# A two-layer block and a second block on one core: gated outputs copied out of PSUM early, decays spread among key projections, sums of squares moved to VectorE, one more value piece ahead of the first transposes

## The chip, the core and the metric

The kernel runs on one core of a Trainium2 chip. Its engines are TensorE (PE in the profile, with its weight loads as PEld), VectorE (DVE), ScalarE (ACT), GpSimd (POOL) and SyncE (SP), which issues most DMAs. Each engine takes its own instructions strictly in order and waits for others by semaphores. The metric is device time in microseconds (us), as a median of several runs.

## The reference

x (512 tokens, 1024 features) goes through two layers of a first block, and then through a second block (windowed attention with a spatial gate, attention over a memory of 256 tokens, a feed-forward part). The change lies in the two layers. Cut to what matters, one layer computes:

```
h = rmsnorm(x);  z = h @ w_in                       # g_q g_k g_v g_lr g_gate  c_q c_kv k_pe  m_gate
log_a = log_sigmoid(g_lr @ w_gate_up + b) / 16      # decays of the gated linear attention (gla)
b = cumsum(log_a) in chunks;  q_dec = q*exp(b);  k_inv = k*exp(-b)
o = causal(q_dec k_inv^T) v + q_dec state           # 4 heads of 64 x 128, state carried from chunk to chunk
o_gla = rmsnorm(o, per head) * silu(g_gate)
q = rmsnorm(c_q) @ w_uq;  k, v = rmsnorm(c_kv) @ w_ukv   # 4 heads, norm per head, rope, causal softmax
o_mla = softmax(q k^T) v * silu(m_gate)
x = x + concat(o_gla, o_mla) @ w_out
```

## The kernel before

Every large product is computed as three fp32r matmuls of a high and a low part (`mm3`, L232 to L234): high by high, low by high, high by low. So every weight is split after its DMA: a ScalarE cast makes the high part (L94, tile whi) and a VectorE subtraction the low part (L95, tile wlo). x is split likewise in `u_chunk` (L360 on ScalarE, L361 on VectorE), which also sums the squares of x over its eight pieces of 128 features: ScalarE squares (L366), and GpSimd adds to `sq` (L367). RMS scales are not applied to x before the product but to its results, so `sq` is only needed when `r_cols` (L378) turns it to one scale per token.

The program is written as one stream, and a scheduler decides from it the order in which each engine's instructions stand, PE's too. What fills PE while a chain of small operations runs elsewhere is handed out by `Fill`: a call runs one piece of a projection (half an output tile, 12 matmuls of 512 columns) and then what is due by `later(d, ...)` after d calls.

Layer 0 begins with `first_proj`: for each of the eight pieces of x, 12 matmuls of 464 columns into four accumulators (three banks of tag s and the one bank of tag o). In the same loop `rope_angles` puts small VectorE operations (L306 to L327) between the pieces. Then `r_cols`, `post_a` (scales and sums of squares of the latents), one value piece, and for each token tile t of 128 tokens `post_b` (the normed latent `cn`, L489 and L491), a value piece and `post_c`, whose transposes (L241) bring the latent of the tile before to feature order. Eight value pieces exist; layer 0 uses five up to here.

Then `queries` for t = 0 to 3 (12 matmuls of 384 columns each; ScalarE's L539 sums squares and frees the bank), with `decays` behind the first (matmul L510, exp L515, log L516, subtraction L518) and value pieces between. Behind the queries of tile t stands `gla_decay(t - 1)`: a matmul with a cumulative mask into the o bank (L613), two exponentials out of it (L615, L616) and a copy (L617). `r_bcast` (L390, copied by L392) spreads the scales. Then `keys` for t = 0 to 3, each two matmul groups into banks of tag s, with pieces of the gla projections between.

`attention` runs the softmax attention (`mla_scores`: matmuls L717 and L720 into two banks of tag s), and inside its fills the gla chunks: `gla_scores`, and one call later `gla_out`, which accumulates into two banks `po` (L666, L672). There are three banks of tag s in all. `po` is squared (L695), reduced (L696), turned to a scale (GpSimd's power, L246), and one call later multiplied out of PSUM (L702); only then are the two banks free.

## Time and profile before

| | |
|---|---|
| median of 3 runs | 1286.16 us (1284.43 to 1286.36) |
| the profiled execution: its time, its span | 1282.27 us, 1280.6 us |
| instructions | 16386 |
| DVE busy | 718.1 us (56%) |
| ACT busy | 519.9 us (41%) |
| POOL busy | 218.6 us (17%) |
| granted TensorE clock, mean | 0.997 |

Shares of busy time are averages over stages with different limits. The chain that ended last lists the lines of `mm3` first, each at 19% of the span. In the view by stretches of 20 us, PE is below 19.99 us busy in the stretches up to 160 us and from 280 to 420 us, at 580, 680, 860 and 880 us, and at the end; these first two ranges are the two layers up to the end of their attention.

### The profile page before, as it was taken

The page shows a single profiled execution, that of the slowest core. Times are in us where ns is not written, and L with a number is a line of the kernel's source. Part 1 is how long each engine was busy: PE and PEld are TensorE (multiplying, and loading weights), DVE is VectorE, ACT ScalarE, POOL GpSimd, SP SyncE. Part 2 cuts the span into 40 slices and gives each one's busy share as a digit, 9 for nine tenths or more (in the row PEclk, how much of TensorE's full clock was granted, in tenths as well). Part 3 has the DMA queues.
Part 4 walks back from the last instruction along what each step waited for, and adds up shares of the span by engine and source line. Part 5 has one row for each costly group of instructions (what it writes and reads, how often), then busy time and mean ns, then how long its engine had stood idle before and what let it go on. Part 6 is the DMA issues. An engine that isn't in the chain of part 4 may idle for free.

```text
span 1280.6 us, 16386 instructions
## 1 busy us (share of the span) xinstructions
PE 1255.0 (98%) x6158; PEld 1020.3 (80%) x6158; DVE 718.1 (56%) x1372; ACT 519.9 (41%) x1174; POOL 218.6 (17%) x247
## 2 busy tenths in 40 slices
PE   8899999999999999999999999999999999999997
PEld 6786678888766888888888888887888888888886
DVE  8666566566656554545376447646655543555532
ACT  6663334456433442215643334445433222333231
POOL 4442001344210141000010002200311100011110
PEclk9999999999999999999999999999999999999999
DMA  6123014513302375221123333323222224332311
GB/s 226 60 100 101 34 33 144 175 46 99 115 1 66 109 229 189 68 98 67 63 78 92 101 95 107 99 99 99 99 86 96 72 90 131 104 97 97 105 48 66
DMA packets 39375, 124.32 MB, mean 97 GB/s; under 512 B 4812, under 2 KB 5862, under 8 KB 39168
## 3 DMA queue, kind: packets, MB, share of 16 engines
q1 hardware_dynamic: 36432, 114.18, 27.4%
q0 software_dynamic: 2576, 8.79, 2.2%
q8 instruction: 48, 0.79, 0.2%
q10 hardware_dynamic: 288, 0.31, 0.1%
q14 instruction: 31, 0.25, 0.1%
HBM read 116.97 MB, written 6.29 MB: 96 GB/s over the span
## 4 chain that ended last, share of the span: by engine, by line
PE 65%; DVE 2%; issue 1%; ACT 1%; POOL 0%; POOLq 0%; ACTq 0%; DVEq 0%
PE psz L232 19%; PE psz L233 19%; PE psz L234 19%; PE pstr L241 1%; PE pss L232 1%; PE pss L234 1%; PE pss L233 1%; PE pss L1142 1%; PE pss L1475 1%; PE pso L755 0%; PE pso L1274 0%; PE pss L717 0%; DVE wlo L95 0%; POOL sm L246 0%; PE pss L1514 0%
## 5 line engine op out<-in xcount | busy, mean ns | idle before, releaser
L94 ACT CAST whi<-wraw 128x512 fp32r<-128x512 f32 (+4 forms) x420 | 226.4, 594 | 311.8 <-PE psz L233 228.0
L95 DVE TENSOR_TENSOR wlo<-wraw,whi 128x512 fp32r<-128x512 f32 (+4 forms) x420 | 298.4, 753 | 70.7 <-ACT whi L94 69.6
L232 PE MATMUL psz<-u,whi 128*128 128x512 f32 x768 | 303.4, 395 | 0.0
L234 PE MATMUL psz<-u,wlo 128*128 128x512 f32 x768 | 299.7, 390 | 0.0
L233 PE MATMUL psz<-u,whi 128*128 128x512 f32 x768 | 299.3, 390 | 0.0
L232 PEld LDWEIGHTS psz<-u,whi 128*128 128x128 f32 x768 | 144.3, 188 | 33.6 <-issue 4.2
L234 PEld LDWEIGHTS psz<-u,wlo 128*128 128x128 f32 x768 | 144.2, 188 | 30.5
L233 PEld LDWEIGHTS psz<-u,whi 128*128 128x128 f32 x768 | 144.3, 188 | 28.5
L232 PE MATMUL psz<-big,whi 128*128 128x512 f32 (+1 forms) x328 | 126.0, 384 | 0.1
L234 PE MATMUL psz<-big,wlo 128*128 128x512 f32 (+1 forms) x328 | 125.1, 381 | 0.0
L233 PE MATMUL psz<-big,whi 128*128 128x512 f32 (+1 forms) x328 | 124.9, 381 | 0.0
L1555 POOL TENSOR_TENSOR t<-t,t 128x512 f32<-128x512 f32 x22 | 34.4, 1561 | 255.2 <-DVE t L1553 242.7
L367 POOL TENSOR_TENSOR t<-t,t 128x512 f32<-128x512 f32 x35 | 49.8, 1422 | 152.2 <-ACT t L366 151.8
L232 PE MATMUL psz<-whi,u 128*128 128x512 f32 (+1 forms) x192 | 75.5, 393 | 0.0
L233 PE MATMUL psz<-wlo,u 128*128 128x512 f32 (+1 forms) x192 | 72.9, 380 | 0.0
L234 PE MATMUL psz<-whi,u 128*128 128x512 f32 (+1 forms) x192 | 72.8, 379 | 0.0
L232 PEld LDWEIGHTS psz<-big,whi 128*128 128x128 f32 x328 | 61.7, 188 | 12.9 <-DVE x L1011 0.5
L233 PEld LDWEIGHTS psz<-big,whi 128*128 128x128 f32 x328 | 61.7, 188 | 12.3 <-issue 0.2
L234 PEld LDWEIGHTS psz<-big,wlo 128*128 128x128 f32 x328 | 61.7, 188 | 12.2
L246 POOL TENSOR_TENSOR sm<-sm,mhalf 128x4 f32<-128x4 f32 (+2 forms) x38 | 35.4, 931 | 165.5 <-DVE sm L697 51.7
L1553 DVE TENSOR_TENSOR t<-psz,Rh 128x512 f32<-128x512 f32 x21 | 14.5, 691 | 66.1 <-PE psz L234 66.1
L1011 DVE TENSOR_TENSOR x<-psz,x 128x512 f32<-128x512 f32 x24 | 16.5, 690 | 54.8 <-PE psz L234 54.8
(361 smaller groups left out, 1894.4 us busy)
## 6 DMA issues: line engine op xcount, KB each, us to landing
wraw<-wts SPq DMA_DIRECT2D x166, 512.0 KB, 4.2
wraw<-wts SPq DMA_DIRECT2D x16, 384.0 KB, 3.2
wraw<-wts SPq DMA_DIRECT2D x16, 352.0 KB, 3.0
x<-t SPq DMA_DIRECT2D x16, 256.0 KB, 3.4
big<-xT SPq DMA_DIRECT2D x8, 256.0 KB, 5.1
t<-xT POOLq DMA_DIRECT2D x8, 256.0 KB, 3.8
t<-x POOLq DMA_DIRECT2D x8, 256.0 KB, 4.2
x<-x SPq DMA_DIRECT2D x8, 256.0 KB, 3.0
```

Of the source, the lines that this page charges most:

```text
L94: nc.scalar.copy(hi, raw)
L95: nc.vector.tensor_tensor(lo, raw, hi.bitcast(F32), ALU.subtract)
L232: mm(out, lhsT[0], rhs[0], start=start, stop=False)
L233: mm(out, lhsT[0], rhs[1], start=False, stop=False)
L234: mm(out, lhsT[1], rhs[0], start=False, stop=stop)
L241: self.nc.tensor.transpose(out, in_, self.ident[0:n, 0:n])
L246: self.nc.gpsimd.tensor_tensor(out, a, self.mhalf[:, 0:n], ALU.pow)
L367: nc.gpsimd.tensor_tensor(self.sq[:], self.sq[:], s[:], ALU.add)
L1011: self.nc.vector.tensor_tensor(x, z[:], x, ALU.add)
L1142: nc.tensor.matmul(dst, qk[b, i, tsl[tt]], qk[b, 2 + i, kc], start=True, stop=True)
L1553: nc.vector.tensor_tensor(up[:], zu[:], Rh[:], ALU.mult)
L1555: nc.gpsimd.tensor_tensor(gt[:], gt[:], up[:], ALU.mult)
```

## The change

There are four edits.

- In `u_chunk` the addition to `sq` goes to VectorE for all pieces in `first_proj`, and for the last piece (k = 7) everywhere; other additions stay on GpSimd.
- `rope_angles` leaves `first_proj`; its operations now stand between the `post_b`/`post_c` of layer 0, and `fill(2)` in place of `fill()` runs two value pieces ahead of the loop, so three run before the first transposes.
- In both layers `gla_decay` leaves the query loop: decay 0 stands behind `r_bcast`, decay 1 behind the key projection of t = 0, decays 2 and 3 behind the next fill.
- In `gla_out` the two accumulators are copied to SBUF at once, one by ScalarE and one by VectorE; square and scaling then read the copy.

```diff
--- before.py
+++ after.py
@@ -350,7 +350,7 @@
         self.ul = [self.ubig(dt=F32R), self.ubig(dt=F32R)]
         self.sq = self.t2()
 
-    def u_chunk(self, k, x, gain):
+    def u_chunk(self, k, x, gain, eng=None):
 
         nc = self.nc
         if k == 0:
@@ -364,7 +364,8 @@
         else:
             s = self.t2()
             nc.scalar.activation(s[:], x, AF.Square)
-            nc.gpsimd.tensor_tensor(self.sq[:], self.sq[:], s[:], ALU.add)
+            eng = nc.vector if k == KD - 1 else eng or nc.gpsimd
+            eng.tensor_tensor(self.sq[:], self.sq[:], s[:], ALU.add)
 
     def u(self, k, cols):
         return (self.uh[k // 4][:, k % 4, cols], self.ul[k // 4][:, k % 4, cols])
@@ -407,13 +408,10 @@
 
         x = self.x
         zs = [self.psum(kind) for kind in "ssso"]
-        angles = self.rope_angles()
         for k, w in enumerate(self.W.with_x(n, x, self.xsrc)):
-            self.u_chunk(k, x[k], gain)
+            self.u_chunk(k, x[k], gain, self.nc.vector)
             if k == 3:
                 self.later_constants()
-            if k > 1:
-                next(angles, None)
             if k == KD - 2:
                 self.W.ahead(2)
             for t in range(NT):
@@ -690,18 +688,16 @@
             L.mid = new
             L.fill.later(1, lambda: self.gla_scores(L, t + 1))
         og = self.lay.tile([P, 4, P], F32, tag="o", name=self.name("og"), bufs=2)
+        nc.scalar.copy(og[:, 0::2, :], po[0][:, 0:2, :])
+        nc.vector.tensor_copy(og[:, 1::2, :], po[1][:, 0:2, :])
         sq, s4, r4 = self.t2((P, 4, P)), self.sm(4), self.sm(4)
-        for par in range(2):
-            nc.scalar.activation(sq[:, 2 * par:2 * par + 2, :], po[par][:, 0:2, :], AF.Square)
+        nc.scalar.activation(sq[:], og[:], AF.Square)
         nc.vector.tensor_reduce(s4[:], sq[:], AX, ALU.add)
         nc.vector.tensor_scalar(s4[:], s4[:], 1.0 / GLA_DV, EPS, ALU.mult, ALU.add)
         self.rsqrt(r4[:], s4[:])
 
         def normed():
-            for par in range(2):
-                nc.vector.tensor_tensor(og[:, par::2, :], po[par][:, 0:2, :],
-                                        r4[:, 2 * par:2 * par + 2, None].to_broadcast([P, 2, P]),
-                                        ALU.mult)
+            nc.vector.tensor_tensor(og[:], og[:], r4[:, :, None].to_broadcast([P, 4, P]), ALU.mult)
             L.o["g", t] = og
             self.gated(L, "g", t)
 
@@ -889,14 +885,18 @@
                 self.post_a(L, t, zs[t])
             L.v = self.big()
             fill.add(vfill)
-            fill()
+            angles = self.rope_angles()
+            fill(2)
             for t in range(NT):
                 self.post_b(L, t)
                 if t:
                     fill()
                     self.post_c(L, t - 1)
+                    next(angles)
             fill()
             self.post_c(L, NT - 1)
+            for _ in angles:
+                pass
             self.rope_tables()
         else:
             units = W.get(2, A_W)
@@ -948,12 +948,11 @@
         L.dec = self.lay.tile([P, NT, 2], F32, tag="dec", name=self.name("dec"))
         for t in range(1, NT):
             self.queries(L, wq, t)
-            self.gla_decay(L, t - 1)
             fill()
-        self.gla_decay(L, NT - 1)
         L.R = self.lay.tile([P, T], F32, tag="Rl", name=self.name("Rl"))
         L.om = self.lay.tile([P, 4, T], F32, tag="om", name=self.name("om"))
         self.r_bcast(L.r, L.R[:])
+        self.gla_decay(L, 0)
         L.kT, L.vm = self.big(), self.big()
         (wkv,) = W.get(1, T, ahead=0)
         rhs = [self.u(k, slice(0, T)) for k in range(KD)]
@@ -962,7 +961,14 @@
         fill.add(self.feat_fill2(rhs, lambda m, z: self.gate_heads(L, m, z)))
         for t in range(NT):
             self.keys(L, wkv, t)
-            fill((2, 1, 1, 3)[t])
+            if t == 0:
+                self.gla_decay(L, 1)
+                fill()
+                self.gla_decay(L, 2)
+                self.gla_decay(L, 3)
+                fill()
+            else:
+                fill((1, 1, 3)[t - 1])
         self.attention(L)
         self.output(L, ("n1", "mix")[l], l)
 
```

VectorE in the first projection of layer 0, from the second to the fourth piece of x (u is the low part of x, wlo that of the weight). Before:

```order
L321 SCALAR_TENSOR_TENSOR sin<-sin,t_24_208 128x4x32
L317 TENSOR_SCALAR cos<-cos 128x4x32
L321 SCALAR_TENSOR_TENSOR sin<-sin 128x4x32
L361 SCALAR_TENSOR_TENSOR u_160<-big_107,gcol,u_158 128x512
L95 TENSOR_TENSOR wlo_133<-wraw_928_139,whi_132 128x464
L321 SCALAR_TENSOR_TENSOR sin<-sin 128x4x32
L318 TENSOR_SCALAR cos<-cos 128x4x32
L361 SCALAR_TENSOR_TENSOR u_160<-big_107,gcol,u_158 128x512
L95 TENSOR_TENSOR wlo_133<-wraw_928_139,whi_132 128x464
```

After (t_20 is `sq`):

```order
L361 SCALAR_TENSOR_TENSOR u_160<-big_107,gcol,u_158 128x512
L95 TENSOR_TENSOR wlo_133<-wraw_0_134,whi_132 128x464
L368 TENSOR_TENSOR t_20_162<-t_20_162,t_21_182 128x512
L361 SCALAR_TENSOR_TENSOR u_160<-big_107,gcol,u_158 128x512
L95 TENSOR_TENSOR wlo_133<-wraw_928_139,whi_132 128x464
L368 TENSOR_TENSOR t_20_162<-t_20_162,t_22_201 128x512
L361 SCALAR_TENSOR_TENSOR u_160<-big_107,gcol,u_158 128x512
L95 TENSOR_TENSOR wlo_133<-wraw_928_139,whi_132 128x464
L368 TENSOR_TENSOR t_20_162<-t_20_162,t_23_220 128x512
```

The rope operations between the pieces are gone, and one addition a piece stands there.

TensorE where `gla_out` of the second token tile meets the scores of attention (L666 and L672, now L664 and L670, fill the accumulators; L717 and L720, now L713 and L716, are the scores). Before:

```order
L680 MATMUL pstr_1385<-big_435,ke_1347 64x128 x4
L717 MATMUL pss_1404<-big_878,big_586 128x256
L720 MATMUL pss_1404<-big_587 128x256
L232 MATMUL psz_1362<-whi_1233,u_159 128x512
L233 MATMUL psz_1362<-wlo_1234,u_159 128x512
L234 MATMUL psz_1362<-whi_1233,u_161 128x512
L232 MATMUL psz_1362<-whi_1233,u_159 128x512
L233 MATMUL psz_1362<-wlo_1234,u_159 128x512
L717 MATMUL pss_1405<-big_878,big_586 128x256
L720 MATMUL pss_1405<-big_587 128x256
```

After:

```order
L678 MATMUL pstr_1385<-big_408,ke_1348 64x128 x4
L713 MATMUL pss_1405<-big_854,big_599 128x256
L713 MATMUL pss_1406<-big_854,big_599 128x256
L716 MATMUL pss_1405<-big_600 128x256
L716 MATMUL pss_1406<-big_600 128x256
L232 MATMUL psz_1362<-whi_1233,u_159 128x512
L233 MATMUL psz_1362<-wlo_1234,u_159 128x512
```

The second score accumulator moves up: before, five matmuls of a projection (psz) stand ahead of it, now none.

ScalarE around the first decay of layer 0 (L516 is the log, L539 the squares of queries, L553 a copy of transposed queries, L615 and L616 the decay's exponentials). Before, from the table load for the log on:

```order
L516 ACT_TABLE_LOAD
L516 ACTIVATE big_623<-big_623 128x1024
L553 COPY big_586<-pstr_670 128x4x128
L539 ACTIVATE t_94_682,sm_681<-pss_683 128x192 x2
L539 ACTIVATE t_94_682,sm_681<-pss_694 128x192
L615 ACT_TABLE_LOAD
L615 ACTIVATE qk_676<-pso_714 128x2x128
L539 ACTIVATE t_94_682,sm_681<-pss_694 128x192
L616 ACTIVATE qk_676<-pso_714 128x2x128
L94 CAST whi_880<-wraw_0_882 128x256
```

After (now L537, L551, L613 and L614; L94 is a weight cast, L393 the copy of the spread scales, L574 and L576 read the key projection of t = 0):

```order
L537 ACTIVATE t_117_798,sm_797<-pss_799 128x192
L94 CAST whi_916<-wraw_0_918 128x512
L537 ACTIVATE t_117_798,sm_797<-pss_810 128x192
L551 COPY big_599<-pstr_834 128x4x128
L537 ACTIVATE t_117_798,sm_797<-pss_810 128x192
L393 COPY Rl_840<-pss_842 128x512
L613 ACT_TABLE_LOAD
L613 ACTIVATE qk_689<-pso_848 128x2x128
L614 ACTIVATE qk_689<-pso_848 128x2x128
L574 ACTIVATE t_136_878<-pss_874 128x256
L576 COPY big_855<-pss_874 128x256
L574 ACTIVATE t_138_886<-pss_882 128x256
```

The first decay's table load and exponentials move from between the queries to behind all of them and behind the copy of the scales, and the readers of the first keys follow at once.

## Rows read from the trace of the kernel before

**Rows 1.** The page, busy us, share of the span and instructions of each engine.
```profile
PE 1255.0 (98%) x6158; PEld 1020.3 (80%) x6158; DVE 718.1 (56%) x1372; ACT 519.9 (41%) x1174; POOL 218.6 (17%) x247
```

**Rows 2.** Waits of PE: line, releaser, us in total, times, longest.
```profile
PE pss L717 <- DVE og L702: 5.4, 5, 1.4
PE pss L233 <- DVE wlo L95: 3.3, 3, 1.7
PE pstr L241 <- DVE t L489: 2.4, 1, 2.4
```

**Rows 3.** Timeline of PE, first projection: start, us, operation, count, idle before and releaser.
```profile
5.75 0.90 PE L232 MATMUL pss<-whi,u 128*128 128x464 f32 x3 [0.65 <-ACT whi L94]
...
13.71 0.48 PE L233 MATMUL pss<-wlo,u 128*128 128x464 f32 x1 [1.71 <-DVE wlo L95]
...
15.50 0.37 PE L232 MATMUL pso<-whi,u 128*128 128x464 f32 x1
...
18.05 0.37 PE L232 MATMUL pso<-whi,u 128*128 128x464 f32 x1
...
30.48 0.95 PE L378 MATMUL pstr<-c,t 128*128 128x1 f32 x8
```

**Rows 4.** Timeline of DVE, third and fourth piece of the first projection.
```profile
10.18 1.85 DVE L361 SCALAR_TENSOR_TENSOR u<-big,gcol,u 128x512 fp32r<-128x512 f32 x1
11.95 1.70 DVE L95 TENSOR_TENSOR wlo<-wraw,whi 128x464 fp32r<-128x464 f32 x1
...
13.92 0.73 DVE L361 SCALAR_TENSOR_TENSOR u<-big,gcol,u 128x512 fp32r<-128x512 f32 x1
14.58 0.62 DVE L95 TENSOR_TENSOR wlo<-wraw,whi 128x464 fp32r<-128x464 f32 x1
```

**Rows 5.** Timeline of POOL, first additions to the sum of squares.
```profile
7.87 5.29 POOL L367 TENSOR_TENSOR t<-t,t 128x512 f32<-128x512 f32 x3 [2.58 <-ACT t L366]
```

**Rows 6.** Timeline of ACT, its last square in the first projection.
```profile
16.87 0.62 ACT L366 ACTIVATE t<-big 128x512 f32<-128x512 f32 x1
```

**Rows 7.** Timeline of PE, value pieces and the first transposes of layer 0.
```profile
31.29 0.48 PE L232 MATMUL psz<-whi,u 128*128 128x512 f32 x1
...
36.87 0.27 PE L241 MATMUL pstr<-c,t 128*65 128x128 f32 x1
...
39.73 0.41 PE L241 MATMUL pstr<-c,t 128*128 128x128 f32 x2 [2.36 <-DVE t L489]
```

**Rows 8.** Timeline of PE, the two waiting decays of layer 0.
```profile
60.36 0.71 PE L613 MATMUL pso<-c,big 128*128 128x130 f32 x4 [1.36 <-DVE big L518]
...
75.47 0.71 PE L613 MATMUL pso<-c,big 128*128 128x130 f32 x4 [0.92 <-DVE halves L617]
```

**Rows 9.** Busy us (and instructions) of PE, PEld, DVE, ACT, POOL, then clock, DMA.
```profile
57.45:73.26 15.81, 14.45 (x89) 12.93 (x88) 10.72 (x26) 14.37 (x46) 9.78 (x14) 1.00 0.27 92
```

**Rows 10.** Timeline of ACT, table load, log, scales, exponential of the last decay.
```profile
56.57 1.28 ACT L516 ACT_TABLE_LOAD   x1
57.86 1.06 ACT L516 ACTIVATE big<-big 128x1024 f32<-128x1024 f32 x1
...
74.33 0.68 ACT L392 COPY Rl<-pss 128x512 f32<-128x512 f32 x1
...
76.22 0.38 ACT L615 ACTIVATE qk<-pso 128x256 f32<-128x256 f32 x1 [0.30 <-PE pso L613]
```

**Rows 11.** Timeline of PE, scores of attention around one gated output, layer 0.
```profile
124.44 0.70 PE L717 MATMUL pss<-big,big 128*128 128x256 f32 x2
...
128.48 0.67 PE L717 MATMUL pss<-big,big 128*128 128x256 f32 x2 [1.36 <-DVE og L702]
```

**Rows 12.** Timeline of DVE, the scaling that frees the second accumulator.
```profile
128.58 0.41 DVE L702 TENSOR_TENSOR og<-pss,sm 128x256 f32<-128x256 f32 x1
```

**Rows 13.** Timeline of ACT, the two squares of the same accumulators.
```profile
123.96 0.66 ACT L695 ACTIVATE t<-pss 128x256 f32<-128x256 f32 x2 [3.77 <-PE pss L672]
```

**Rows 14.** PE busy, granted clock and DMA in four us behind that wait.
```profile
130.00:134.00 4.00, 4.00 (x19) 0.57 0.01 4
```

## The prediction

> **What bounds the kernel now.** I read the page first, then the waits of PE, then each engine's timeline at the places of those waits. On the page PE is busy for 98% of the span [rows 1] and no engine beside it for more than 56%, so a change on another engine is worth only what PE waits less, or more. The waits of PE name the places: 5.4 us before score matmuls, for the scaling of the gated outputs; 3.3 us for the low part of a weight; 2.4 us for the first normed latent [rows 2]; and two single waits of 1.36 and 0.92 us in front of decays [rows 8]. Together these are 13.4 us, 1.0% of the span. All lie in the two layers, and each of the four edits is aimed at one of them. In the stretch of the queries PE is not alone: in 15.81 us ScalarE is busy for 14.37 us and PE for 14.45 us [rows 9]. There a moved instruction can cost as much as it saves.
>
> The profiled execution took 1282.27 us, 1.67 us more than its span; the median of the three timed runs is 3.9 us above it. I make the sum against the profiled execution and take its difference from the median.
>
> **First projection.** The first matmul starts at 5.75 and the column sums of squares at 30.48 us [rows 3], so eight pieces take 24.73 us. Between the waits a piece needs 2.55 us: the same matmul of two successive pieces starts at 15.50 and at 18.05 [rows 3]. Eight such pieces are 20.4 us, so 4.3 us are lost, of which the listed wait of 1.71 us is the largest part. Its cause is on VectorE: the two splits of the third piece take 1.85 and 1.70 us, those of the fourth 0.73 and 0.62 us [rows 4]; GpSimd works on three additions from 7.87 to 13.16 us [rows 5], over the long pair and not over the short one. The edit takes that neighbour away and adds one operation of 512 columns on two SBUF inputs. I price it as the split of x, 0.73 us [rows 4]; a piece then costs VectorE 0.73 + 0.62 + 0.73 = 2.1 us, less than PE's 2.55 us, without the rope operations. ScalarE does not bind: its last square begins at 16.87 us [rows 6], when PE still has pieces left. About 0.3 us at the first low part stay. Gain 4.0 us, between 3.0 and 4.3. If the additions run at 1.85 us, there is no gain but a loss (the slower rival).
>
> The other additions of the last piece (both layers' outputs and the two later blocks) are worth nothing: no wait on the column sums stands among those of PE [rows 2], and each moves one operation of 0.73 us to VectorE. The rope operations become a load of VectorE among the latents, under PE's value pieces; if that cover fails they can delay a transpose by up to 1 us, so I keep 0 to -1.
>
> **One more value piece.** The first value matmul starts at 31.29 and the first transpose at 36.87 us, so a piece of 12 matmuls takes 2.79 us; the normed latent comes 2.36 us late [rows 7]. With a third piece ahead the transpose is asked for 2.79 us later, so the wait goes, with 0.4 us to spare even if the chain behind the column sums stays as long. Gain 2.4 us, between 1.5 and 2.6. The piece is not new work; it is missing later, among the queries.
>
> **Decays.** The two waits in front of decays go: 2.3 us [rows 8]. What is late next is ScalarE. From the end of the second queries PE has one value piece left as cover, where it had two in before: PE's 14.45 us of work lose 2.79 us and three decays, each about 0.5 us of the 0.71 us of its record [rows 8]: some 10.2 us are left. ScalarE's 14.37 us lose the decays' table load of 1.28 us [rows 10] and six exponentials at about 0.4 us [rows 10]: 10.7 us are left. So the two are level, the three banks of tag s hand over only as fast as ScalarE squares, and every in-order hand-over costs PE something. I take 2.5 us of new waits up to the second key projection. Behind it the new order holds decay 1 back: its bank is free only after ScalarE's copy of the scales (0.68), the table load (1.28) and two exponentials (0.38 each) [rows 10], together 2.7 us; meanwhile PE has decay 0 (0.5 us) and nine matmuls, six of the first key projection and three of the next piece, at 0.23 us each (2.79 / 12): 2.6 us. With 0.4 us for the hand-overs and 0.5 us that ScalarE is late with the query squares, both estimates of mine, a wait of 1.0 us is left. In layer 0 this makes -3.5 + 2.3 = -1.2 us, between +2.3 (no new wait) and -4. In layer 1 no such wait went before; the value pieces there still stand between the queries, so only the wait at decay 1 arises, without the three matmuls (0.7 us) as cover and without ScalarE's lateness: 2.7 + 0.4 - 1.9 = 1.2 us, so -1.2 us, between 0 and -2.5.
>
> In the trace a table load takes 1.28 us and the log behind it starts at once, at 57.86 after 56.57 + 1.28 [rows 10]. The Trainium skill (ScalarE: Activation LUTs, What ACT_TABLE_LOAD costs) gives about 1.28 us for the load and about 1.38 us more for a drain, 2.66 us for each switch; by that the wait at decay 1 would be 1.4 us longer in each layer, and the sum below 2.8 us smaller. The trace agrees with its first figure and not with the second.
>
> **Gated outputs.** The five waits of 5.4 us [rows 2] come from one pattern. Of three banks two are held by the gated output; the second score accumulator waits until the scaling has read one: the first scores start at 124.44, the second pair at 128.48 after a wait of 1.36 us [rows 11], when the scaling is about to read the other bank [rows 12]. The squares read the same accumulators at 123.96 and need 0.66 us for both [rows 13]; a copy of one by ScalarE is half of that, 0.33 us, so the bank is free by about 124.3 us, and VectorE's copy, priced as its 0.41 us of scaling [rows 12], a little later. The second scores, now right behind the first, want it at about 124.9 us. So the wait goes wherever the copy is first in its queue. At the last token tile a layer's weight casts and splits stand ahead of the copies; I leave 0.6 us there. Square and scaling now start later by a copy, about 0.4 us, which nothing notices: the output's transposes come a full round later. Gain 5.4 - 0.6 = 4.8 us, between 3 and 5.4.
>
> Behind one of these waits the granted clock is 0.57 in the mean over four us [rows 14], so most of it ran at 1.2 and not 2.4 GHz: 4 x 0.43 = 1.7 us lost. PE had stood still shortly before. Without the wait I expect full clock there: 1.7 us, or 0 if the cause lies elsewhere; a loss of the same size can arise if the new waits of layer 0 lie close together.
>
> **Sum.** 4.0 + 2.4 - 1.2 - 1.2 + 4.8 + 1.7 = 10.5 us. The profiled execution becomes 1271.8 us, the median 1286.16 - 10.5 = 1275.7 us.
>
> **Rivals.**
> - ScalarE takes back what the decays give. For it: 14.37 of 15.81 us [rows 9], and a decay chain that now begins behind everything else. Against it: three exponential pairs and a table load leave that stretch. With the lower ends there (-4 and -2.5 in place of -1.2 and -1.2) and the clock's 1.7 us not won, the sum is 4.7 us: 1281.5 us. A table switch of 2.66 us, as the page says, would alone give 7.7 us and 1278.5 us; this lies between. Chance 0.17.
> - No new wait arises. The scheduler's order fits ScalarE's work into the gaps: 4.3 + 2.6 + 2.3 + 0 + 5.4 + 1.7 = 16.3 us, 1269.9 us. Against it: the level load of rows 9. Chance 0.10.
> - Slower: VectorE becomes the bound of the first projection. If its splits were long not because of GpSimd but by themselves (two SBUF inputs), and the additions like them, a piece would cost 1.85 + 1.70 + 1.85 = 5.4 us against PE's 2.55 us, and seven pieces would take 20 us longer than PE's own pace, 16 us longer than before; with the other terms (+6.5) the time is 1295.7 us. It decides from the point where the three pass 2.55 us together. Against it: the short pair [rows 4] lies two microseconds behind the long one, on operands of the same shape. Chance 0.04.
>
> **Chances and range.** The forecast, a gain from 7 to 13 us, gets 0.69. Within 0.2% (2.6 us) is what a measurement of this kernel can't tell from no change. Faster by more takes the forecast, no new wait and nearly all of the ScalarE rival: 0.92. The same: 0.04, from the rest of that rival. Slower: 0.04. The range of 8 in 10 reaches from near the case without new waits, 1270.5 us, to the ScalarE rival, 1282 us.
>
> **What would show it.** In the profile of after: the column sums of squares start at about 26.4 us and no GpSimd addition stands before them; the two splits stay at 0.73 and 0.62 us in all pieces. The wait for the first normed latent is gone. Waits of PE for ScalarE appear between the second queries and the second key projection of layer 0, and one of about a microsecond at decay 1 in each layer. The waits of scores on the gated outputs are gone but for the last tile, and the clock is full behind them. I would be wrong if the first projection ended later than 27.5 us, if waits for ScalarE in the queries passed 5 us, or if score matmuls waited for the copies at every tile.

## The result, and the profile after

The changed kernel takes 1267.38 us (median of 4 runs, 1266.93 to 1268.23) against 1286.23 us before (4 runs, 1284.43 to 1286.36): a ratio of 0.9857, 95% interval 0.984 to 0.9875. The forecast was 1275.7 us, in a range from 1270.5 to 1282.0: the sign was right, the gain of 18.9 us was larger than the 10.5 forecast, and the time lies below the range. The profiled execution took 1267.09 us with a span of 1265.4 us, so the spans differ by 15.2 us and the medians by 3.7 us more.

The page after, busy us and share of the span (answers [rows 1]), and the granted TensorE clock in 40 slices, in tenths:

```profile
PE 1247.6 (99%) x6158; PEld 1019.0 (81%) x6158; DVE 717.6 (57%) x1383; ACT 521.4 (41%) x1174; POOL 201.3 (16%) x236
...
PEclk9999999999999999999999999999999999999999
```

PE executes as many matmuls as before and is busy for 99% of the span, but its busy time fell by 7.4 us. So about half of the gain isn't idle time that went: 1.7 us of it is the stretch at a lower clock [rows 14], and for the rest some of the same matmuls became shorter. That is the first sign of what the forecast lacked.

The waits of PE after: line, releaser, us in total, times, longest (answers [rows 2] and [rows 8]).

```profile
PE pso L611 <- DVE halves L615: 2.9, 3, 1.0
...
PE pstr L241 <- ACT t L742: 1.0, 3, 0.4
PE pstr L241 <- DVE t L534: 0.9, 1, 0.9
PE pstr L241 <- POOL t L1027: 0.8, 1, 0.8
PE pstr L241 <- DVE sm L540: 0.7, 1, 0.7
```

All three waits of [rows 2] are gone. At the decays, three waits for the copy that frees their bank (L615) stand where one stood before [rows 8], and three waits of 0.7 to 0.9 us at the transposes of the queries are new.

To see where the 15.2 us lie, I compare the start of one and the same instruction in both traces of PE: the column sums of squares, the first and the last score group of each layer, and the end. A score group is the score matmuls of one pair of heads and one token tile; the last one of a layer counts with the stage behind it.

| PE instruction | before | after | gain of the stage up to it |
|---|---|---|---|
| column sums, layer 0 | 30.48 | 26.16 | 4.3 (first projection) |
| first scores, layer 0 | 103.60 | 99.47 | -0.2 (latents, queries, keys) |
| last scores, layer 0 | 185.30 | 174.88 | 6.3 (attention) |
| first scores, layer 1 | 331.05 | 321.75 | -1.1 (output, latents, queries, keys) |
| last scores, layer 1 | 411.50 | 396.44 | 5.8 (attention) |
| span | 1280.6 | 1265.4 | 0.1 (the rest) |

The forecast had 4.0, 1.2, 6.5 for both attentions with the clock, and -1.2. So the attentions hold the surprise: 12.05 us in place of 6.5. There the score matmuls after stand as follows (PE, layer 0, the token tile of [rows 11], 256 columns):

```profile
120.05 1.13 PE L713 MATMUL pss<-big,big 128*128 128x256 f32 x4
121.11 0.70 PE L716 MATMUL pss<-big 64*128 64x256 f32 x4
121.75 0.50 PE L232 MATMUL psz<-whi,u 128*128 128x512 f32 x1
```

The two heads of a pair now stand together: wide products of both, then the 64-row products of both. From start to start this takes 1.06 + 0.64 = 1.70 us. Before, each head's part had stood alone, in this tile from 124.44 and again from 128.48 us [rows 11]; the rows that follow these two are:

```profile
125.07 0.70 PE L720 MATMUL pss<-big 64*128 64x256 f32 x2
125.70 0.50 PE L232 MATMUL psz<-whi,u 128*128 128x512 f32 x1
...
129.08 0.70 PE L720 MATMUL pss<-big 64*128 64x256 f32 x2
129.71 0.50 PE L234 MATMUL psz<-whi,u 128*128 128x512 f32 x1
```

The two parts are 1.26 and 1.23 us long (0.63 + 0.63 and 0.60 + 0.63 us of wide and 64-row matmuls), together 2.49 us without the wait. Over both layers the score groups fill 38.1 us of PE before, where 8 of 16 pairs were split, and 31.9 us after, where none is (the expectations below have 38.2 and 32.0): 6.2 us that no list of waits shows. Of these, 5.4 us lie in the 64-row matmuls (17.2 to 11.8 us) and 0.8 us in the wide ones (20.9 to 20.1 us).

### The profile page after: what moved, and what is told of

It is laid out like the page before. It is cut to its first block, busy times and chain, and to the rows that moved or that the text cites. A ratio compares the mean times of both kernels' runs of the same rounds, so it can differ in the third digit from the quotient of the medians.

```text
span 1265.4 us, 16362 instructions
## 1 busy us (share of the span) xinstructions
PE 1247.6 (99%) x6158; PEld 1019.0 (81%) x6158; DVE 717.6 (57%) x1383; ACT 521.4 (41%) x1174; POOL 201.3 (16%) x236
## 4 chain that ended last, share of the span: by engine, by line
PE 66%; DVE 2%; issue 1%; ACT 1%; POOL 0%; POOLq 0%; DVEq 0%; ACTq 0%
PE psz L232 19%; PE psz L233 19%; PE psz L234 19%; PE pstr L241 1%; PE pss L232 1%; PE pss L234 1%; PE pss L233 1%; PE pss L1481 1%; PE pss L1148 1%; PE pso L1280 0%; PE pso L751 0%; PE psz L1520 0%; POOL sm L246 0%; PE pss L1520 0%; PE pss L713 0%
## 5 line engine op out<-in xcount | busy, mean ns | idle before, releaser
L94 ACT CAST whi<-wraw 128x512 fp32r<-128x512 f32 (+4 forms) x420 | 226.8, 594 | 303.1 <-PE psz L233 230.6
L95 DVE TENSOR_TENSOR wlo<-wraw,whi 128x512 fp32r<-128x512 f32 (+4 forms) x420 | 293.2, 741 | 69.8 <-ACT whi L94 69.0
L1561 POOL TENSOR_TENSOR t<-t,t 128x512 f32<-128x512 f32 x22 | 34.4, 1566 | 255.1 <-DVE t L1559 242.6
L368 POOL TENSOR_TENSOR t<-t,t 128x512 f32<-128x512 f32 x24 | 32.3, 1345 | 138.0 <-ACT t L366 138.0
```

Of the source, the lines that this page charges most:

```text
L94: nc.scalar.copy(hi, raw)
L95: nc.vector.tensor_tensor(lo, raw, hi.bitcast(F32), ALU.subtract)
L368: eng.tensor_tensor(self.sq[:], self.sq[:], s[:], ALU.add)
L1561: nc.gpsimd.tensor_tensor(gt[:], gt[:], up[:], ALU.mult)
```

## The experiments

Three sets of runs were made, each with the kernel before beside it (medians 1283.95, 1284.3 and 1284.11 us); ratios are to these, with 95% intervals. The changed kernel itself was not run again in these sets, so a difference to its 1267.38 us goes from one set to another; where it matters, the traces are compared too. The stages are those of the table above, as gains of the profiled execution against the one before.

| kernel | median us | first proj. | up to scores 0 | attention 0 | up to scores 1 | attention 1 | all |
|---|---|---|---|---|---|---|---|
| as changed | 1267.38 | 4.3 | -0.2 | 6.3 | -1.1 | 5.8 | 15.2 |
| copies alone | 1272.11 | 0.0 | -3.2 | 5.4 | 0.0 | 5.8 | 8.2 |
| heads apart | 1278.97 | 3.4 | -0.2 | 1.7 | -2.6 | 1.5 | 2.6 |
| same half | 1272.98 | 4.0 | -0.1 | 4.2 | -1.9 | 3.9 | 9.3 |
| additions alone | 1277.33 | 3.5 | 2.5 | -0.4 | 0.0 | -1.5 | 4.0 |
| rope operations alone | 1281.54 | 3.2 | 0.1 | -0.2 | 0.1 | -0.1 | 3.2 |
| value piece alone | 1281.48 | -0.1 | 1.7 | -0.1 | 0.0 | -1.6 | -0.1 |
| decays back | 1264.36 | 4.3 | 1.6 | 6.1 | 0.2 | 5.8 | 18.1 |
| one piece | 1265.08 | 3.6 | 2.2 | 6.4 | -1.2 | 5.8 | 16.9 |
| one piece, decays later | 1264.16 | 4.0 | 2.0 | 6.3 | 0.2 | 5.7 | 18.5 |
| one piece, decays apart | 1264.15 | 3.6 | 2.2 | 6.3 | -0.3 | 5.8 | 17.8 |
| by layer | 1263.64 | 4.4 | 2.2 | 6.2 | 0.2 | 5.8 | 18.8 |

With equal code the first projection varies by up to 1 us between executions (3.4 to 4.4 us where additions and rope operations are as changed), so differences below 1 us in "all" say little.

**Copies alone.** The kernel before with the edit of `gla_out` only.

```diff
+        nc.scalar.copy(og[:, 0::2, :], po[0][:, 0:2, :])
+        nc.vector.tensor_copy(og[:, 1::2, :], po[1][:, 0:2, :])
...
-            nc.scalar.activation(sq[:, 2 * par:2 * par + 2, :], po[par][:, 0:2, :], AF.Square)
+        nc.scalar.activation(sq[:], og[:], AF.Square)
...
```

> The kernel before with the copies of the gated outputs alone. Theory: against the trace of before, the changed kernel gains 6.7 us in the attention of layer 0 and 6.1 us in that of layer 1, 12.8 us, where the prediction had 4.8 + 1.7 = 6.5 us; half of it is no wait but the two score products of a head pair, which stand next to each other once both accumulators are free (38.2 us of score matmuls before, 32.0 us after). So 1286.2 - 12.8 = 1273.4 us, with no score pair split and the waits for the scaling gone. Rival, the prediction's size: 1286.2 - 6.5 = 1279.7 us, and the rest belongs to other edits.

1272.11 us, ratio 0.9905 (0.9885 to 0.9925), 11.8 us below before and nearer to the theory than to the rival. The waits for the scaling are gone and the score groups fill 31.9 us. So 11.2 of the attentions' 12.05 us belong to this edit; the other 0.9 us, in layer 0, are small differences, one of them a wait of 0.3 us on another reader (L728). In this trace, 3.2 us are lost far ahead of the edit, behind the wait for the first normed latent that this kernel still has. That wait, and PE's clock in a window behind it (window, length, busy, clock, DMA share, GB/s):

```profile
PE pstr L241 <- DVE t L489: 2.8, 1, 2.8
...
40.00:44.00 4.00, 3.85 (x11) 0.50 0.40 132
```

0.50 is the lower of the two levels, 1.2 GHz. In the profiled execution of before the same wait stood, and the clock stayed full behind it.

**Heads apart.** The changed kernel with the four score matmuls of a pair issued head by head.

```diff
             nc.tensor.matmul(s[:, 0:n], L.qT[:, h, ts], L.kT[:, h, 0:n], start=True, stop=False)
-        for par, s in enumerate(ss):
             b = slice(64 * par, 64 * par + 64)
             nc.tensor.matmul(s[:, 0:n], L.rT[b, hp, ts], L.rT[b, 2 + hp, 0:n],
```

> The changed kernel with the score matmuls of a head pair issued head by head (wide and 64-row product of one head, then of the other) instead of both wide ones and then both 64-row ones. Work and banks are the same. Theory: next to each other the two 64-row products take the time of one (0.63 us for four of 256 columns after, 0.63 us for two before), and the wide ones lose less to switching; by the rows of before the pairs become longer by 0.67 us (128 columns), 0.79 (256) and about 0.9 (384), four of each, and by about 1.3 us (512, estimated from the others), in all 14.6 us: 1267.4 + 14.6 = 1282.0 us, with no new wait of PE. Rival: the score matmuls were only long because something else stood between them or PE had waited; then the order of four adjacent matmuls does nothing: 1267.4 us.

1278.97 us, ratio 0.996 (0.9945 to 0.9975): 11.6 us above the changed kernel, with the same instructions and no wait for a gated output. The same tile as above (PE):

```profile
122.23 0.70 PE L713 MATMUL pss<-big,big 128*128 128x256 f32 x2
122.86 0.70 PE L715 MATMUL pss<-big 64*128 64x256 f32 x2
123.49 0.70 PE L713 MATMUL pss<-big,big 128*128 128x256 f32 x2
124.12 0.70 PE L715 MATMUL pss<-big 64*128 64x256 f32 x2
124.74 0.50 PE L232 MATMUL psz<-whi,u 128*128 128x512 f32 x1
```

2.51 us in place of 1.70. The score groups fill 46.2 us, 14.3 us more than after, close to the 14.6 estimated; the median is only 11.6 us longer, so 2.7 us come back elsewhere (the waits on L742, 1.0 us, are gone). The rival falls: order alone is worth this much.

**Same half.** The changed kernel with both 64-row products on rows 0 to 63.

```diff
-            b = slice(64 * par, 64 * par + 64)
+            b = slice(0, 64)
```

> The changed kernel with the 64-row score product of odd heads read from rows 0 to 63 as for even heads (it leaves out the odd heads' own rope part, rows 64 to 127); the order of instructions is the same. Theory: two 64-row products next to each other take the time of one because they lie on different halves of the array's rows; on the same half they run one after the other and a group of four takes as long as the wide group (0.54, 1.06, 1.4 and 1.8 us for 128 to 512 columns in place of 0.42, 0.64, 0.85 and 1.06), four groups of each size: 4 x 1.85 = 7.4 us more, 1274.8 us. Rival: what counts is only that products of one shape stand together; then nothing changes: 1267.4 us.

1272.98 us, ratio 0.991 (0.9895 to 0.9925), 5.6 us above the changed kernel, where the theory had 7.4. A tile of 256 columns (PE, layer 1):

```profile
342.42 1.13 PE L713 MATMUL pss<-big,big 128*128 128x256 f32 x4
343.49 1.13 PE L716 MATMUL pss<-big 64*128 64x256 f32 x4
344.54 0.50 PE L232 MATMUL psz<-whi,u 128*128 128x512 f32 x1
```

The 64-row group takes 1.05 us here and 0.64 us when its heads lie on different halves; at 512 columns 1.91 and 1.06. The wide matmuls take as long as after (20.1 us in all); the 64-row ones fill 20.4 us in place of 11.8, 8.5 us more, of which 2.9 us do not show in the median (the waits on L742, 1.0 us, are gone again). So two 64-row products run side by side if they follow each other on different halves of the rows, and the rival falls. That is most of what the splitting of pairs had cost, 5.4 of 6.2 us. The Trainium skill (TensorEngine Tiling (Array Packing), Key Properties) says that tiles of the array work independently of each other, and that a change of the tiling mode drains the array. The traces agree with the first, side by side above. They fit the second, though no row shows a drain as such: the wide product of one head that stands alone between 64-row ones (heads apart) takes 0.63 us from start to start, against 0.53 (1.06 for two) in the joined group, where two heads share one change of mode.

**Additions alone.** The kernel before with the additions to `sq` on VectorE.

```diff
-            nc.gpsimd.tensor_tensor(self.sq[:], self.sq[:], s[:], ALU.add)
+            eng = nc.vector if k == KD - 1 else eng or nc.gpsimd
+            eng.tensor_tensor(self.sq[:], self.sq[:], s[:], ALU.add)
...
-            self.u_chunk(k, x[k], gain)
+            self.u_chunk(k, x[k], gain, self.nc.vector)
```

> The kernel before with the additions to the sum of squares on VectorE (all pieces of the first projection, the last piece elsewhere); the rope operations stay between the pieces. Theory, the prediction's cause: the splits of the third piece were long (1.85 and 1.70 us) because GpSimd added beside them, so they fall to 0.73 and 0.62 us, the wait of 1.7 us goes, and the column sums start some 3 to 4 us earlier than at 30.48; the time is about 3.5 us below before. Rival: the rope operations, small but ahead of each split in VectorE's queue, cost the time; then the wait stays and the column sums start at 30 us or later, since VectorE has one more operation a piece.

1277.33 us, ratio 0.9943 (0.9928 to 0.9958). The column sums start at 26.98 us; VectorE's third piece and the first reading of the sums:

```profile
9.29 0.75 DVE L361 SCALAR_TENSOR_TENSOR u<-big,gcol,u 128x512 fp32r<-128x512 f32 x1
9.95 0.64 DVE L95 TENSOR_TENSOR wlo<-wraw,whi 128x464 fp32r<-128x464 f32 x1
10.50 0.69 DVE L368 TENSOR_TENSOR t<-t,t 128x512 f32<-128x512 f32 x1
...
27.96 0.16 DVE L382 TENSOR_SCALAR sm<-pstr 128x4 f32<-128x4 f32 x1 [0.45 <-PE pstr L379]
```

The theory holds, and the gain is larger than forecast for this edit: the wait for the first normed latent (2.4 us) is gone too, with one value piece ahead as before. VectorE reads the column sums 0.98 us after they start; before it was 2.89 us (30.48 to 33.37), because two pairs of weight splits that wait for casts stood in its queue ahead of the reading (VectorE, before):

```profile
30.32 1.29 DVE L95 TENSOR_TENSOR wlo<-wraw,whi 128x512 fp32r<-128x512 f32 x2 [0.76 <-ACT whi L94]
32.03 1.29 DVE L95 TENSOR_TENSOR wlo<-wraw,whi 128x512 fp32r<-128x512 f32 x2 [0.42 <-ACT whi L94]
...
33.37 0.15 DVE L381 TENSOR_SCALAR sm<-pstr 128x4 f32<-128x4 f32 x1
```

Why the reading stands earlier in that queue with this edit is not shown.

**Rope operations alone.** The kernel before with `rope_angles` moved to the latents.

```diff
-        angles = self.rope_angles()
...
-            if k > 1:
-                next(angles, None)
...
+            angles = self.rope_angles()
             fill()
...
                     self.post_c(L, t - 1)
+                    next(angles)
...
```

> The kernel before with the rope operations alone moved out of the first projection to the latents; the additions stay on GpSimd. Theory: the additions alone gave the earlier column sums (26.98 against 30.48 us) and the end of the wait for the first normed latent, so the rope operations are worth little: the column sums at 29 to 30.5 us, the time within 1.5 us of before. Rival: GpSimd's additions are only harmful together with the rope operations, which read and write SBUF on VectorE beside them; then moving either is enough, the column sums come at about 27 us and the time is 5 us or more below before.

1281.54 us, ratio 0.9979 (0.9968 to 0.999). The theory was wrong for the projection: the column sums start at 27.26 us. VectorE beside GpSimd's additions:

```profile
9.39 1.74 DVE L95 TENSOR_TENSOR wlo<-wraw,whi 128x464 fp32r<-128x464 f32 x1
11.05 1.79 DVE L361 SCALAR_TENSOR_TENSOR u<-big,gcol,u 128x512 fp32r<-128x512 f32 x1
12.76 0.63 DVE L95 TENSOR_TENSOR wlo<-wraw,whi 128x464 fp32r<-128x464 f32 x1
...
30.01 0.15 DVE L381 TENSOR_SCALAR sm<-pstr 128x4 f32<-128x4 f32 x1
```

The splits stay long beside the additions, yet PE waits for a low part once, for 0.6 us, where before it was 3.3 us in three waits: without the rope operations VectorE has room for long splits. It took both to make VectorE late, and taking away either is enough there (3.2 and 3.5 us, together 4.3). But the sums are read 2.75 us after they start, and the wait for the normed latent stays (2.2 us). So the rival holds for the projection and falls for the time.

**Value piece alone.** The kernel before with a second piece.

```diff
             fill.add(vfill)
-            fill()
+            fill(2)
```

> The kernel before with two value pieces in place of one ahead of the transposes' loop, nothing else. Theory: the wait of 2.4 us for the first normed latent goes, but the piece is missing among the later queries, where about 2.3 us of waits come up, so the trace is about as long as before; the half clock that one execution showed behind that wait (0.50 from 40 to 44 us with the copies alone) cannot come, so the median may be up to 2 us below before. Prediction's term: 2.4 us below before in the trace as well, since the piece is not missed.

1281.48 us, ratio 0.9978 (0.9966 to 0.999), 2.6 us below before. In the trace 1.7 us are gained up to the first scores, less than the 2.4 of the prediction's term and more than the theory's nothing. The same trace then loses 1.6 us in the attention of layer 1, at half clock, where before had lost none (columns as with the copies alone; the first line is layer 0, the second layer 1):

```profile
128.00:132.00 4.00, 4.00 (x14) 0.57 0.02 4
364.00:368.00 4.00, 4.00 (x19) 0.59 0.00 0
```

**Decays back** and **one piece.** The changed kernel with the decays behind the queries as before; and the changed kernel with one value piece ahead.

```diff
             self.queries(L, wq, t)
+            self.gla_decay(L, t - 1)
             fill()
+        self.gla_decay(L, NT - 1)
...
-            if t == 0:
-                self.gla_decay(L, 1)
...
+            fill((2, 1, 1, 3)[t])
```

```diff
-            fill(2)
+            fill()
```

> The changed kernel with the decays back behind the queries as before; all other edits stay. Theory: by the traces aligned at equal work the moved decays lose 3.1 us in layer 0 (waits of 0.9 to 1.0 us for the copy of the last decay and three between the queries) and 1.1 us in layer 1: 1267.4 - 4.2 = 1263.2 us. Rival, the waits among the queries of layer 0 come from the value piece that is missing there, not from the decays: then only the two or three waits at decays go (2.9 us) and the two of before (1.36 and 0.92 us) return, 1267.4 - 0.6 = 1266.8 us.

> The changed kernel with one value piece ahead of the transposes' loop instead of two; all other edits stay. Theory: the third piece is worth 2.7 us at the first transpose, but 2.4 us of waits stand where it is missing, among the later queries (0.88, 0.78 and 0.73 us): 1267.4 + 2.7 - 2.4 = 1267.7 us, no difference. Rival, the prediction's sum: the piece is worth its 2.4 us and the queries' waits have another cause: 1269.8 us.

1264.36 us (ratio 0.9844, 0.9826 to 0.9861) and 1265.08 us (0.9848, 0.9827 to 0.9869), so each is 2 to 3 us faster than the changed kernel (spans 2.9 and 1.7 us shorter). For the decays the theory was nearer than the rival; for the piece both were wrong: it isn't worth 2.4 us, and it isn't worth nothing, it costs 2.3. The first transposes with one piece ahead (PE):

```profile
33.25 0.27 PE L241 MATMUL pstr<-c,t 128*65 128x128 f32 x1
...
34.23 0.41 PE L241 MATMUL pstr<-c,t 128*128 128x128 f32 x2 [0.48 <-DVE t L487]
```

Only 0.48 us of the 2.36 us [rows 7] were left for the piece to save. The four combinations, gain up to the first scores of layer 0:

| | one piece ahead | two |
|---|---|---|
| decays behind the queries | 2.5 (additions alone; rope operations still in the projection) | 1.6 (decays back) |
| decays moved | 2.2 (one piece) | -0.2 (as changed) |

Moving the piece costs 0.9 us, moving the decays 0.3 us, both together 2.7 us. The first corner differs from the others by the rope operations too, so the 0.9 and the 0.3 hold what these do among the latents; the steps from the other two corners to the last, 1.8 and 2.4 us, are single edits. The three waits of 0.7 to 0.9 us at the transposes of the queries stand only with both: with the decays back one of 0.3 us is left of them, with one piece none. Each edit takes cover from the same later queries, and the second one finds too little left.

**One piece with other places for the decays.** Each decay one place later than before (behind the third and fourth queries, the scales, the first keys); as changed, but decays 2 and 3 set apart by a piece and a key projection; and "by layer", layer 0 as changed and layer 1 one place later. The first two as diffs against one piece:

```diff
             self.queries(L, wq, t)
+            if t > 1:
+                self.gla_decay(L, t - 2)
             fill()
...
-        self.gla_decay(L, 0)
+        self.gla_decay(L, 2)
...
+            if t == 0:
+                self.gla_decay(L, 3)
+            fill((2, 1, 1, 3)[t])
```

```diff
                 self.gla_decay(L, 1)
                 fill()
                 self.gla_decay(L, 2)
-                self.gla_decay(L, 3)
-                fill()
             else:
-                fill((1, 1, 3)[t - 1])
+                if t == 1:
+                    self.gla_decay(L, 3)
+                fill((2, 1, 3)[t - 1])
```

> The changed kernel with one value piece ahead and with each decay one place behind that of the kernel before: decay 0 behind the third queries, decay 1 behind the fourth, decay 2 behind the spreading of the scales, decay 3 behind the first key projection. Theory: with one value piece ahead the time was 1265.1 us, of which 2.7 us are waits of decays on the copy of the decay ahead of them (three waits, decays too close together); with a fill between any two decays they go and the first log has time to end: 1262.4 us. Rival: ScalarE has no room between the queries, its exponentials and table loads there delay the query squares by what the waits gave: 1265 us.

> The changed kernel with one value piece ahead and decays 0 and 1 as changed, but decay 2 behind the first piece after the first keys and decay 3 behind the second keys. Theory: of the three waits of decays (2.7 us) the two that follow a decay with little between go, the one of decay 1 behind the first keys stays: 1265.1 - 1.7 = 1263.4 us in sum over both layers. Rival: a decay's wait depends on ScalarE being busy with the keys, not on the distance, and they stay: 1265.1 us.

> The changed kernel with one value piece ahead; in layer 0 the decays as changed, in layer 1 each one place behind that of the kernel before (0 and 1 behind the third and fourth queries, 2 behind the spread scales, 3 behind the first keys). Theory: the best part of each layer in the traces so far: layer 0 up to attention gains 2.2 us against before with the decays as changed (2.0 one place later, 1.6 as before), layer 1 gains 0.2 us one place later where it loses 1.2 us as changed; so 1265.1 - 1.4 = 1263.7 us, level with the best so far (1264.15) or a little below. Rival: the two layers are not independent and it is no better than one value piece alone, 1265.1 us.

1264.16 us (0.9842, 0.9827 to 0.9857), 1264.15 us (0.9841, 0.9824 to 0.9857) and 1263.64 us (0.9845, 0.983 to 0.9861). The first gained less than its theory: the decays' waits fall from 2.7 to 0.7 us, but others come (0.8 us for a weight's low part, 0.6 us for ScalarE's work on the keys). In the second the theory fails in its reason: the decays' waits are still there,

```profile
PE pso L611 <- DVE halves L615: 3.0, 3, 1.2
```

and the 0.9 us of the median come from layer 1 (-0.3 in place of -1.2 us). "By layer" is the sum of the best stages, as expected, 3.7 us below the changed kernel's median, and the fastest of all; its lead of 0.5 us over the other two is too small to tell.

## Why the prediction was wrong, step by step

**The step that failed: gated outputs.** "So the wait goes wherever the copy is first in its queue", worth "5.4 - 0.6 = 4.8 us", and 1.7 us for the clock. The mechanism was right and the waits went, but the sum priced only the waiting. What moved on PE was seen in the order (the second score accumulator moves up to the first) and priced at nothing, as if a matmul took the same time wherever it stands. Measured: waits for the scaling 5.4 us and for the softmax behind it 0.5 us, score groups 38.1 - 31.9 = 6.2 us, clock 1.7 us: 13.8 us, of which about 1.8 us come back, 1.2 of it as small waits at transposes, on L742 and on the low part of a split (L455). That leaves the 12.05 us of the two stages against 6.5. Heads apart and same half show the 6.2 us for what they are. At the last tile no wait of 0.6 us was left.

**First projection.** 4.3 us against 4.0 (3.4 to 4.4 with equal code), the column sums at 26.16 against 26.4, the splits at 0.74 and 0.63 us. The cause given, GpSimd's additions, was half of it: the rope operations, priced at nothing, would have given 3.2 us alone.

**One more value piece.** "So the wait goes, with 0.4 us to spare even if the chain behind the column sums stays as long. Gain 2.4 us". It did not stay as long: the additions' edit shortened it by 1.9 us and took the wait first. The wait stands in the sum once, but under the wrong edit: the additions alone gave 3.5 + 2.5 us, nearly the 4.0 + 2.4 us that the sum has for both edits, and behind them the piece only costs.

**Decays, layer 0.** Three waits between the queries (0.9, 0.8 and 0.7 us) and two at decays (0.97 and 0.94) are 4.3 us; the prediction had 3.5 with one at a decay. It named ScalarE as the late engine among the queries. The releasers there are VectorE's products of the queries (L534; for the third wait the view names L540, which stands between these products and which the transposes do not read) and GpSimd's rope of them (L1027). Neither products nor rope read ScalarE's squares. Ahead of the first wait VectorE is busy without a gap; the decays' subtractions (L516) and four weight splits stand before the products:

```profile
54.68 3.39 DVE L516 TENSOR_TENSOR big<-big,big 128x256 f32<-128x256 f32 x4 [0.50 <-ACT big L514]
57.99 0.75 DVE L95 TENSOR_TENSOR wlo<-wraw,whi 128x256 fp32r<-128x256 f32 x2
...
59.61 0.41 DVE L534 TENSOR_TENSOR t<-pss,gqk 128x256 f32<-128x256 f32 x1
```

Ahead of the third, VectorE stands 0.93 us before a weight split, for a cast that itself waited 1.25 us for its weight's DMA. The wait at the second of the two decays (0.94) is ScalarE's, behind the exponentials of the decay ahead of it, and the sum had none there. Piece and decays together: 1.2 us forecast, -0.2 measured.

**Decays, layer 1.** -1.2 forecast, -1.1 measured, by the wait worked out. In layer 0 the chain reads on ScalarE and PE:

```profile
66.37 0.61 PE L611 MATMUL pso<-c,big 128*128 128x130 f32 x4
...
67.47 0.62 ACT L393 COPY Rl<-pss 128x512 f32<-128x512 f32 x1
68.10 1.28 ACT L613 ACT_TABLE_LOAD   x1
69.39 0.38 ACT L613 ACTIVATE qk<-pso 128x256 f32<-128x256 f32 x1
69.67 0.38 ACT L614 ACTIVATE qk<-pso 128x256 f32<-128x256 f32 x1
...
70.30 0.71 PE L611 MATMUL pso<-c,big 128*128 128x130 f32 x4 [0.97 <-DVE halves L615]
```

Scales, table load and two exponentials in a row, and decay 1 waits 0.97 us (0.98 in layer 1), where 1.0 and 1.2 were forecast. In layer 0 that is partly luck: from the start of decay 0 on PE the chain took 3.93 us, not 3.6 (the copy of the scales begins 1.10 us late, not 0.5; the hand-over is 0.25 us, not 0.4), and PE's cover was 2.96 us, not 2.6, so two misses cancel.

The differences add up: 0.3 (projection) - 1.4 (value piece and decays of layer 0) + 0.1 (layer 1) + 5.55 (attentions) + 0.1 (rest) = 4.7 us more than 10.5, the 15.2 us of the spans.

**From the span to the median.** The sum was made on the profiled execution and taken off the median, 3.9 us above it; that difference was assumed to stay. After it is 0.3 us. The medians of before were 1284 to 1286 us, 2 to 4 us above its profiled execution, with runs from 1281.0 to 1286.6; the changed kernel's runs lie within 1.3 us. The traces offer a cause. In the five kernels that keep the waits of [rows 2] on gated outputs or on the normed latent, the clock is low in one or two stretches of the layers, a loss of 1.7 to 3.4 us, not always in the same places; in the eight others, with no wait for gated outputs and at most 0.5 us for the latent, it is full throughout the layers. Before's profiled execution had one such stretch (1.7 us). The timed runs bear this out: of before's 34 runs beside the experiments, the five with a mean granted clock of 0.994 took 1286.2 us in the mean, the fifteen at 0.997 (as in the profiled execution) 1283.1 us, the one at 0.998 1281.0 us, and 0.003 of 1280 us is 3.8 us. The eight kernels without those waits list 0.998 or 0.999 in every run. So most of what before's timed runs lie above its trace goes with a lower clock; behind which waits it fell there is not shown, as they left no trace.

**Rivals.** "No new wait arises" lies nearest in time (1269.9) and is wrong in its reason, since the new waits came. ScalarE took back about a microsecond more than forecast, at the second waiting decay of layer 0, far from that rival's 1281.5 us; VectorE did not become the bound. None of the three conditions named for being wrong came about: they guarded the steps that held, and none asked whether matmuls would change their length.

## What to carry to other kernels

When a change lets matmuls stand together that stood apart, compare their rows as a group, from the start of the first to the start of what follows: a pair of 64-row products on different halves of the rows costs half as much together as apart, and neither a list of waits nor a count of instructions shows it. A wait that two edits could remove can be gained only once, so ask which of them removes it first. Two edits that take cover from the same place can together cost more than the sum of what each costs: run the four combinations before keeping both. A profiled execution on the fast side of its own runs is a sign of something that varies from run to run, and a change that removes it can be worth more in the median than in the trace.

## What the runs showed of the hardware

- Two fp32 products of 64 rows and 256 columns on different halves of the array's rows take 0.64 us from start to start, on the same half 1.05 us; with 512 columns 1.06 and 1.91 us.
- A VectorE operation with two SBUF inputs of 512 or 464 columns takes 0.63 to 0.75 us alone and 1.7 to 1.9 us beside GpSimd's additions of SBUF tiles (with the rope operations alone one took 1.28 and one 2.37 us). The Trainium skill (SBUF — State Buffer, Who interferes with whom) says that a VectorE instruction with two SBUF inputs contends with a GpSimd instruction that reads SBUF; the rope operations alone and the additions alone show it with these numbers.
- In the layers of five kernels the granted clock fell to 1.2 GHz seven times, and each time PE had just waited (1.4 us for a gated output) or was waiting (2.8 us for the latent, with the copies alone). The reverse does not hold: of the eight waits of 1.4 us that are the first long ones of their layer six were followed by such a stretch, of the eight second ones (1.1 to 1.4 us) none, and the waits of 2.4 and 2.2 us for the latent (before, rope operations alone) were not.
